# Causal mask of the attention scores: from accumulating mask products on TensorE to an add within VectorE's row maximum, with the score products of the two maps issued alternately

## The chip, the core and the metric

The kernel runs on one core of a Trainium2 chip. A core has a TensorE for matrix products (PE in the profile; its weight loads are PEld), a VectorE (DVE), a ScalarE (ACT), a GpSimd (POOL) and a SyncE (SP), which here issues most DMAs. Each engine takes its own instructions in order, and engines wait for one another by semaphores. Products land in PSUM, eight banks of 512 fp32 columns on 128 partitions; everything else lies in SBUF. The metric is the device time of one execution in microseconds, the median of several runs.

## What is computed

Two layers of a block over 256 tokens of 1024 features. Each layer has a mixer with three branches (spatial gating, a state space scan, differential attention), which are gated and merged, and a feed forward with a convolution. The change lies in the attention branch, four heads with two score maps each:

```python
def diff_attention(q, k, v, q_g, k_g, lam_vecs, subln_g, lam_init, cos, sin):
    ...
    def block(args):
        qb, bi = args
        scores = jnp.einsum('bqhmd,bkhmd->bhmqk', qb, kh)
        q_pos = bi * Q_BLOCK + jnp.arange(Q_BLOCK)
        mask = k_pos[None, :] <= q_pos[:, None]
        p = jax.nn.softmax(jnp.where(mask, scores, -jnp.inf), axis=-1)
        w = p[:, :, 0] - lam * p[:, :, 1]
        return jnp.einsum('bhqk,bkhd->bqhd', w, vf)
```

A head has 64 features in each map; queries are taken in two blocks of 128. The first block sees keys 0 to 127, the second keys 0 to 255, and in both only the last 128 x 128 square needs the causal mask.

## The kernel before

All weights stream through SBUF in half blocks of 128 x 1024 fp32. ScalarE writes the high part of each (`whi`, L231), VectorE the rest (`wlo`, L234), and every product with weights is three products of such parts (`mm3`, L276 to L278). `next_half` keeps four split half blocks ahead of the one in use; five buffers exist for each part. TensorE goes through the items of a layer in a fixed order: q, k, x B C, v, z, g, u, then gates and branches a, c and b (tiles `g_a`, `b_a`, `g_c`, `b_c`, `g_b`, `b_b`), the output projection (`wo`), and the feed forward (`up`, `acc`).

Everything that is not a stream of weights is written as a generator, whose steps are taken at each half block (`tick`), so many per half block as its rate says. `attention()` is one of them (rate 1.45). It runs beside the gates and branches, together with the state space scan `ssd()` (tiles `seg`, `y`, `xs`) and the spatial gating (`gm`, `gmy`). The framework then orders the instructions of each engine, so the order on an engine can differ a little from that of the text.

Attention goes through five stages for each head, and in one round of the loop at L650 a later stage of an earlier head comes before an earlier stage of a later head:

- `scores` (L581): for each map `m` and each query block a product of 64 rows of `qT` and `kT` into the PSUM tile of that map, columns 0 to 127 for the first block and 128 to 383 for the second. Map 0 lies on partitions 0 to 63 and map 1 on 64 to 127. Directly behind each product a second one, of `identb` (a bf16 identity) and `negb` (0 or -3e38, bf16), adds the mask to the last 128 columns (L590). TensorE takes an fp32 product in two passes, each with its weight load.
- `soft` (L593): VectorE takes four row maxima out of PSUM (L602) and scales them (L603); ScalarE takes four exponentials from PSUM into the SBUF tiles `pe` (L607), each with a row sum.
- `combine` (L613): VectorE makes p0 - lam * p1 with the sums (L617 to L624), in place in `pe`.
- `turn` (L630): TensorE turns three 128 x 128 squares of `pe` (tile `wt`, L633), ScalarE copies them out.
- `values` (L637): TensorE multiplies with `va` (tile `po`).

The `pe` tiles come from a ring of seven buffers of 2 KB (`s2`), which wT, gmy and others share. The PSUM tiles come from a ring of eight banks.

`identb` and `negb` are cast from the constants `cst` once, at the start (L406, L407). `cst` has 592 columns, the mask 128 of them (`K_NEG`).

Of the kernel before, what the change touches and what calls it, by code (L numbers as in the profile page):

```python
# [20 lines left out]
P = 128  # L21
# [9 lines left out]
# order of the mixer's input products: q, k, v, spatial gate g, u, x B C in pairs of tiles, z  # L31
MIX = ("q", "k", "x4", "x5", "v", "x0", "x1", "z0", "x2", "x3", "z1", "g", "u0", "u1")
# buffers of 4 KiB, of 2 KiB and of the split weights
NS4, NS2, NWB, AHEAD = 18, 7, 5, 4
HP = 200
# feed forward: hidden tile after which the down products start
# [7 lines left out]
# columns of w_in  # L44
# [3 lines left out]
# row constants of a layer  # L48
R_GMG, R_GMB, R_SSG, R_DTB, R_D, R_QK, R_SUB = 0, 512, 1024, 2048, 2064, 2080, 2208
R_N = 2336  # L50
# per-partition constants of a layer
PC_CW, PC_CB, PC_FW, PC_FB = 0, 48, 60, 60 + 6 * NFT
PC_N = PC_FB + 2 * NFT
# gains of the input norms, per layer: mixer, feed forward
G_N = 16
# constants that depend on shapes alone
K_ID, K_TRI, K_NEG, K_CC, K_SS = 0, 128, 256, 384, 416
K_II, K_REV = 448, 464
K_N = 592


def feat_block(w, c0, c1):
    """[1024, cols c0:c0+128 and c1:c1+128] -> [128, 2 tiles, 8 k, 128]"""
    a = w.reshape(8, P, -1)
    return np.stack([a[:, :, c : c + P].transpose(1, 0, 2) for c in (c0, c1)], 1).reshape(P, BLK)


def tok_blocks(w):
    """[K, 512 n] -> blocks of [128, 4 k, 512], the k halves of a column group together"""
    k, n = w.shape  # L70
    a = w.reshape(k // 512, 4, P, n // 512, 512).transpose(3, 0, 2, 1, 4)
    return list(a.reshape(-1, P, BLK))


def out_blocks(w):
    """[1024, 1024] -> blocks of [128, 4 tiles, 4 k, 128], halves of k outermost"""
    a = w.reshape(2, 4, P, 2, 4, P).transpose(0, 3, 2, 4, 1, 5)
    return list(a.reshape(-1, P, BLK))
# [41 lines left out]
def bc(ap, n):  # L120
    """append a broadcast dim of n"""
    return ap.unsqueeze(len(ap.shape)).to_broadcast([*ap.shape, n])
# [3 lines left out]
def block_kernel(ctx: ExitStack, tc: tile.TileContext, x, wstream, wdt, rows, prol, pcols, gains, gmw, consts, out):  # L126
# [20 lines left out]
    # the residual stream, features on partitions  # L147
# [13 lines left out]
    # the activation table is there before the data  # L161
# [3 lines left out]
    # the tensor engine's clock is up when the data comes  # L165
# [5 lines left out]

    identb = cpool.tile([P, P], BF16, name="identb")
    negb = cpool.tile([P, P], BF16, name="negb")
# [8 lines left out]
    def prologue():  # L182
        """lambda and -exp(a_log) of both layers"""
        nc.sync.dma_start(pr, prol.rearrange("(o l) f -> o l f", o=1).to_broadcast([P, L, 272]))
        for l in range(L):
            lv = pr[:, l, 0:256].rearrange("p (a b d) -> p a b d", a=2, b=2)
            nc.vector.tensor_tensor(lprod[:, 2 * l : 2 * l + 2, :], lv[:, :, 0, :], lv[:, :, 1, :], op=ALU.mult)
        nc.vector.tensor_reduce(lsum.rearrange("p l a -> p (l a)"), lprod, op=ALU.add, axis=AX.X)
        nc.scalar.activation(lexp, lsum, AF.Exp)
        nc.scalar.activation(aneg, pr[:, :, 256:272], AF.Exp)  # L190
        nc.vector.tensor_scalar(aneg, aneg, -1.0, None, op0=ALU.mult)
        nc.vector.tensor_tensor(neglam, lexp[:, :, 1], lexp[:, :, 0], op=ALU.subtract)
        for l in range(L):
            lam_init = 0.8 - 0.6 * math.exp(-0.3 * l)
            nc.vector.tensor_scalar(neglam[:, l : l + 1], neglam[:, l : l + 1], -lam_init, None, op0=ALU.add)

# [5 lines left out]
    def load_half():  # L202
        i, hf = divmod(stream["i"], 2)
        parts = 1
        if hf == 0:
            raw = wpool.tile([P, BLK], F32, tag="raw", name=f"raw{i}", bufs=3)
            if i == 0:
                # the first block and the tiles of x as they are needed
                for q in range(4):
                    cs = slice(q * 512, (q + 1) * 512)  # L210
                    nc.sync.dma_start(x_sb[:, 2 * q : 2 * q + 2, :], x[:, 2 * q : 2 * q + 2, :])
                    nc.sync.dma_start(raw[:, cs], wstream[i, :, cs])
            elif i == 1:
                for q in range(2):
                    cs = slice(q * HB, (q + 1) * HB)
                    nc.sync.dma_start(raw[:, cs], wstream[i, :, cs])
                nc.sync.dma_start(cst, consts)
            else:
                nc.sync.dma_start(raw, wstream[i])
            stream["raw"] = raw  # L220
# [17 lines left out]
    def next_half():  # L238
        """the next half block; those after it are split ahead"""
        while len(ready) <= AHEAD and stream["i"] < n_halves:  # L240
            load_half()
        return ready.popleft()
# [3 lines left out]
    def load_table(name):  # L246
        """the next activations in program order, with their table set in place"""
        table["ins"] = tc.keep_in_program_order(nc.scalar.preload_act_table_set(name)).ins

# [24 lines left out]
    def mm3(o, a_hi, a_lo, b_hi, b_lo, start, stop):  # L274
        """o += a.T @ b, operands as high + low parts of 12 bits"""
# [4 lines left out]
    def feat_half(o, h_hi, h_lo):  # L280
        """one tile of 128 features of h @ w, features on partitions: o [128, 256]"""
# [6 lines left out]
    def feat_pair(o, h_hi, h_lo):  # L288
        """two tiles, with the last features of h as late as can be"""
# [12 lines left out]
    def tok_group(name, act, nk, evac, between=None):  # L302
        """512 columns of a product, tokens on partitions: act(k, i) gives the high and low
        activations of token tile i, evac(i, psum) takes what comes out"""
# [14 lines left out]
    def rsqrt_mean(src, n, scale, name):  # L319
        """(src * scale + eps) ** -0.5"""  # L320
# [15 lines left out]
    def transpose_split(src, dst, name, nk, scale=1.0):  # L336
        """src [128 tokens, nk * 128] -> features on partitions, high and low parts;
        dst(k0, k1) gives where tiles k0 to k1 go"""
# [14 lines left out]
    def scaled_tile(k, g, h_hi, h_lo):  # L353
        """feature tile k of x times its gain, split; the norm's factor of a token is applied to
        what the products give"""
# [10 lines left out]
    def norm_factors(name, res):  # L366
        """1 / rms of x by token: res gets [128, 2] with tokens on partitions, half of it, and the
        same along a row"""
# [35 lines left out]
    def layer_constants(l):  # L404
        if l == 0:
            nc.vector.tensor_copy(identb, ident)  # L406
            nc.vector.tensor_copy(negb, cst[:, K_NEG : K_NEG + P])  # L407
# [23 lines left out]
    for l in range(L):  # L431
# [34 lines left out]
        def dt_raw():  # L466
# [20 lines left out]
            # one table set for both functions  # L487
# [3 lines left out]
            # softplus(x) = max(x, 0) + log1p(exp(-|x|))  # L491
# [8 lines left out]
            # what rounding 1 + e dropped, to first order  # L500
# [10 lines left out]
            # cumulative sums within chunks: by token, by head, and what is left to the end of chunk 0  # L511
# [63 lines left out]
        def attention():  # L575
# [5 lines left out]
            def scores(h):  # L581
                sc[h] = []
                for m in range(2):
                    o = ps(f"sc{l}_{h}_{m}")
                    ms = slice(64 * m, 64 * m + 64)
                    for i, (c0, n) in enumerate(spans):
                        nc.tensor.matmul(  # L587
                            o[:, c0 : c0 + n], qT[ms, h, i * P : (i + 1) * P], kT[ms, h, 0:n], start=True, stop=False
                        )
                        nc.tensor.matmul(o[:, c0 + n - P : c0 + n], identb, negb, start=False, stop=True)  # L590
                    sc[h].append(o)

            def soft(h):  # L593
                # columns: (tile 0, map 0), (tile 0, map 1), (tile 1, map 0), (tile 1, map 1)
# [4 lines left out]
                for m in range(2):  # L599
                    for i, (c0, n) in enumerate(spans):  # L600
                        q = 2 * i + m
                        nc.vector.tensor_reduce(mx[:, q : q + 1], sc[h][m][:, c0 : c0 + n], op=ALU.max, axis=AX.X)  # L602
                nc.vector.tensor_scalar(nmx, mx, -0.125, None, op0=ALU.mult)  # L603
                for m in range(2):
                    for i, (c0, n) in enumerate(spans):
                        q = 2 * i + m
                        nc.scalar.activation(  # L607
                            p[m][:, c0 : c0 + n], sc[h][m][:, c0 : c0 + n], AF.Exp,
# [4 lines left out]
            def combine(h):  # L613
                # weights over sum 0: p0 - lam * (sum0 / sum1) * p1
# [60 lines left out]
        def normed(o, row, name):  # L675
            """two feature tiles times the norm's factors"""
# [43 lines left out]
        def conv(u, y, wcol, bcol, taps, pcl):  # L720
            """causal depthwise convolution along the free axis"""
# [13 lines left out]
        def ssd_in():  # L735
            # B with tokens on partitions
# [7 lines left out]
            # C B^T, lower triangle, transposed  # L744
# [12 lines left out]
        def x_tokens(b):  # L757
            """half the heads with tokens on partitions: x, dt x, the skip term, and what chunk 0
            leaves to chunk 1"""
# [59 lines left out]
        def ssd():  # L819
# [13 lines left out]
            def decay(i, g):  # L833
                # exp(min(a_t - a_s, 0))
# [82 lines left out]
        # what can go beside the stream once these items are there  # L917
# [25 lines left out]
        # a gate is (tanh(x / 2) + 1) / 2; the half is taken where the merged sum is split  # L943
# [130 lines left out]
def shape_constants():  # L1074
# [6 lines left out]
    c[:, K_NEG : K_NEG + P] = np.where(r[None, :] <= r[:, None], 0.0, -3.0e38)  # L1081
# [77 lines left out]
```

## Time and profile before

| what | value |
|---|---|
| median of 3 runs | 973.7 us (973.24 to 974.42) |
| profiled execution: span from the first to the last instruction | 970.6 us |
| profiled execution: its own time beside the span | not listed; the median of the runs is 3.1 us above the span |
| instructions | 15931 |
| TensorE clock granted, mean | 0.998 |
| DMA | 172.71 MB, 178 GB/s over the span |

The page gives the busy time of each engine, the costliest groups of instructions with what ended the idle time before them, and the chain of work that ended last: followed back from the last instruction, at each step to what released it, or to the instruction before it on its engine. The time of the chain is what the kernel takes; idle time of an engine off the chain costs nothing. Ends of products are modelled, so the distance from start to start says more than a product's own duration. The chain can be read piece by piece in order of time, and its pieces are such distances.

### The profile page before, as it was taken

How to read it: one execution, taken by the hardware profiler on the slowest of the kernel's cores; microseconds unless marked ns; L12 is line 12 of the kernel's file. 1: busy time of each engine (PE TensorE's matmuls, PEld its weight loads, DVE VectorE, ACT ScalarE, POOL GpSimd, SP SyncE). 2: the span in 40 equal slices, each digit the busy share in tenths (PEclk: the TensorE clock that was granted, in tenths of full speed). 3: DMA queues.
4: the chain of work that ended last, by engine and by line, in shares of the span. 5: the costliest groups of instructions: out<-in, count | busy, mean ns of one | idle time of the engine just before them, and what ended most of it. 6: DMA issues, size and time to landing. Idle time of an engine off the chain costs nothing.

```text
span 970.6 us, 15931 instructions
## 1 busy us (share of the span) xinstructions
PE 961.9 (99%) x6465; PEld 877.5 (90%) x6465; DVE 714.7 (74%) x1072; ACT 572.9 (59%) x880; POOL 39.3 (4%) x48
## 2 busy tenths in 40 slices
PE   8999999999999999999999999999999999999998
PEld 5999787888899999999988988878888999999998
DVE  6698767667568978787677975776756788877774
ACT  6676577554445755555457666776544566555552
POOL 2020010000000000000001100000000000000000
PEclk9999999999999999999999999999999999999999
DMA  7854572347555555555544555633455545555541
GB/s 294 277 178 174 174 260 99 131 141 243 186 174 174 175 187 194 184 177 177 190 177 151 175 175 174 234 113 131 158 189 175 178 169 198 193 175 177 186 160 44
DMA packets 29145, 172.71 MB, mean 178 GB/s; under 512 B 5232, under 2 KB 6544, under 8 KB 9360
## 3 DMA queue, kind: packets, MB, share of 16 engines
q1 hardware_dynamic: 27712, 167.46, 49.9%
q0 software_dynamic: 1216, 4.23, 1.4%
q8 instruction: 50, 0.82, 0.3%
q14 instruction: 23, 0.19, 0.1%
q10 hardware_dynamic: 144, 0.02, 0.0%
HBM read 170.61 MB, written 1.08 MB: 177 GB/s over the span
## 4 chain that ended last, share of the span: by engine, by line
PE 98%; DMA 0%; POOL 0%; ACT 0%; DVE 0%; issue 0%; ACTq 0%; POOLq 0%
PE up L276 9%; PE up L277 9%; PE up L278 9%; PE acc L278 4%; PE acc L277 4%; PE acc L276 4%; PE xbc L276 2%; PE xbc L277 2%; PE xbc L278 2%; PE sc L587 2%; PE wo L278 2%; PE wo L277 2%; PE wo L276 2%; PE g_a L276 2%; PE g_a L277 2%; PE g_a L278 2%
## 5 line engine op out<-in xcount | busy, mean ns | idle before, releaser
L231 ACT ACTIVATE whi<-raw 128x1024 fp32r<-128x1024 f32 (+1 forms) x310 | 325.0, 1051 | 274.8 <-PE up L277 82.4
L234 DVE TENSOR_TENSOR wlo<-raw,whi 128x1024 fp32r<-128x1024 f32 (+1 forms) x310 | 375.8, 1216 | 148.1 <-ACT whi L231 145.5
L276 PE MATMUL up<-f_hi,whi 128*128 128x256 f32 x704 | 199.6, 283 | 0.0
L277 PE MATMUL up<-f_lo,whi 128*128 128x256 f32 x704 | 199.2, 283 | 0.0
L278 PE MATMUL up<-f_hi,wlo 128*128 128x256 f32 x704 | 199.2, 283 | 0.0
L277 PEld LDWEIGHTS up<-f_lo,whi 128*128 128x128 f32 x704 | 135.2, 192 | 0.0
L276 PEld LDWEIGHTS up<-f_hi,whi 128*128 128x128 f32 x704 | 135.2, 192 | 0.0
L278 PEld LDWEIGHTS up<-f_hi,wlo 128*128 128x128 f32 x704 | 135.1, 192 | 0.0
L276 PE MATMUL acc<-act,whi 128*128 128x256 f32 x352 | 99.6, 283 | 0.0
L277 PE MATMUL acc<-act,whi 128*128 128x256 f32 x352 | 99.6, 283 | 0.0
L278 PE MATMUL acc<-act,wlo 128*128 128x256 f32 x352 | 99.6, 283 | 0.0
L727 DVE SCALAR_TENSOR_TENSOR fy<-fu,pc,fy 128x254 f32<-128x254 f32 (+1 forms) x176 | 73.6, 478 | 0.2
L276 PEld LDWEIGHTS acc<-act,whi 128*128 128x128 f32 x352 | 67.6, 192 | 0.0
L277 PEld LDWEIGHTS acc<-act,whi 128*128 128x128 f32 x352 | 67.6, 192 | 0.0
L278 PEld LDWEIGHTS acc<-act,wlo 128*128 128x128 f32 x352 | 67.6, 192 | 0.0
L276 PE MATMUL xbc<-h_hi,whi 128*128 128x256 f32 x192 | 55.1, 287 | 0.0
L277 PE MATMUL xbc<-h_lo,whi 128*128 128x256 f32 x192 | 54.3, 283 | 0.0
L278 PE MATMUL xbc<-h_hi,wlo 128*128 128x256 f32 x192 | 54.3, 283 | 0.0
L722 ACT ACTIVATE fy<-fu,pc 128x256 f32<-128x256 f32 x88 | 47.7, 588 | 3.8 <-DVE fu L678 3.8
L328 ACT ACTIVATE act<-fy 128x256 fp32r<-128x256 f32 x44 | 18.3, 416 | 49.3 <-DVE fy L1023 49.3
L678 DVE TENSOR_TENSOR fu<-up,fn_row 128x512 f32<-128x512 f32 x44 | 30.2, 690 | 16.0 <-PE up L278 16.0
L277 PEld LDWEIGHTS xbc<-h_lo,whi 128*128 128x128 f32 x192 | 36.8, 192 | 0.1
(305 smaller groups left out, 1970.9 us busy)
## 6 DMA issues: line engine op xcount, KB each, us to landing
raw<-in_wstream SPq DMA_DIRECT2D x152, 1024.0 KB, 4.9
seg<-scr POOLq DMA_DIRECT2D x8, 512.0 KB, 7.0
rows<-in_rows SPq DMA_DIRECT2D x2, 1168.0 KB, 7.9
x_sb<-in_x SPq DMA_DIRECT2D x4, 256.0 KB, 4.5
raw<-in_wstream SPq DMA_DIRECT2D x4, 256.0 KB, 4.7
raw<-in_wstream SPq DMA_DIRECT2D x2, 512.0 KB, 6.7
out_x<-x_sb SPq DMA_DIRECT2D x8, 128.0 KB, 1.8
gmw<-in_gmw SPq DMA_DIRECT2D x2, 256.0 KB, 6.0
```

The costliest lines, as they stand in the source:

```text
L231: split = nc.scalar.activation(hi[:, cs], src[:, cs], AF.Copy)
L234: nc.vector.tensor_tensor(lo[:, cs], src[:, cs], hi[:, cs].bitcast(F32), op=ALU.subtract)
L276: nc.tensor.matmul(o, a_hi, b_hi, start=start, stop=False)
L277: nc.tensor.matmul(o, a_hi, b_lo, start=False, stop=False)
L278: nc.tensor.matmul(o, a_lo, b_hi, start=False, stop=stop)
L328: nc.scalar.activation(dst_hi, src, AF.Copy, scale=scale)
L587: nc.tensor.matmul(o[:, c0 : c0 + n], qT[ms, h, i * P : (i + 1) * P], kT[ms, h, 0:n], start=True, stop=False)
L678: nc.vector.tensor_tensor(u, o.rearrange("p (m t) -> p m t", m=2), row.unsqueeze(1).to_broadcast([P, 2, S]), op=ALU.mult)
L722: nc.scalar.activation(y, u, AF.Identity, bias=pcl[:, bcol : bcol + 1], scale=pcl[:, wcol + taps - 1 : wcol + taps])
L727: nc.vector.scalar_tensor_tensor(y[:, d:], u[:, : S - d], pcl[:, w : w + 1], y[:, d:], op0=ALU.mult, op1=ALU.add)
```

## The change

The mask products and their two bf16 constants go. The score products are ordered by query block first and map second, so that successive products take map 0 and map 1 in turn; each is a complete product by itself. VectorE's row maximum becomes `tensor_tensor_reduce`: it reads the scores from PSUM and the mask from SBUF, writes their sum to the `pe` tile, and gives its row maximum (scale 1.0, start value -3e38). The exponential reads the `pe` tile and writes over it. The mask in the constants is 256 columns wide, 128 of zero and then the triangle, so that one slice of it fits either query block; `cst` grows from 592 to 720 columns. Comments are removed everywhere, which changes nothing that runs.

```diff
-K_ID, K_TRI, K_NEG, K_CC, K_SS = 0, 128, 256, 384, 416
-K_II, K_REV = 448, 464
-K_N = 592
+K_ID, K_TRI, K_NEG, K_CC, K_SS = 0, 128, 256, 512, 544
+K_II, K_REV = 576, 592
+K_N = 720
...
-    identb = cpool.tile([P, P], BF16, name="identb")
-    negb = cpool.tile([P, P], BF16, name="negb")
...
-        if l == 0:
-            nc.vector.tensor_copy(identb, ident)
-            nc.vector.tensor_copy(negb, cst[:, K_NEG : K_NEG + P])
...
             def scores(h):
-                sc[h] = []
-                for m in range(2):
-                    o = ps(f"sc{l}_{h}_{m}")
-                    ms = slice(64 * m, 64 * m + 64)
-                    for i, (c0, n) in enumerate(spans):
+                sc[h] = [ps(f"sc{l}_{h}_{m}") for m in range(2)]
+                for i, (c0, n) in enumerate(spans):
+                    for m in range(2):
+                        ms = slice(64 * m, 64 * m + 64)
                         nc.tensor.matmul(
-                            o[:, c0 : c0 + n], qT[ms, h, i * P : (i + 1) * P], kT[ms, h, 0:n], start=True, stop=False
+                            sc[h][m][:, c0 : c0 + n], qT[ms, h, i * P : (i + 1) * P], kT[ms, h, 0:n],
+                            start=True, stop=True,
                         )
-                        nc.tensor.matmul(o[:, c0 + n - P : c0 + n], identb, negb, start=False, stop=True)
-                    sc[h].append(o)
...
-                        nc.vector.tensor_reduce(mx[:, q : q + 1], sc[h][m][:, c0 : c0 + n], op=ALU.max, axis=AX.X)
+                        nc.vector.tensor_tensor_reduce(
+                            p[m][:, c0 : c0 + n], sc[h][m][:, c0 : c0 + n], cst[:, K_NEG + 2 * P - n : K_NEG + 2 * P],
+                            1.0, -3.0e38, op0=ALU.add, op1=ALU.max, accum_out=mx[:, q : q + 1],
+                        )
...
-                            p[m][:, c0 : c0 + n], sc[h][m][:, c0 : c0 + n], AF.Exp,
+                            p[m][:, c0 : c0 + n], p[m][:, c0 : c0 + n], AF.Exp,
                             bias=nmx[:, q : q + 1], scale=0.125, accum_out=sums[:, q : q + 1],
...
-    c[:, K_NEG : K_NEG + P] = np.where(r[None, :] <= r[:, None], 0.0, -3.0e38)
+    c[:, K_NEG + P : K_NEG + 2 * P] = np.where(r[None, :] <= r[:, None], 0.0, -3.0e38)
```

## The prediction

> **What bounds the kernel now.** I read the busy table of the page and the summary of the chain that ended last, then all waits of TensorE.
>
> ```profile
> PE 961.9 (99%) x6465; PEld 877.5 (90%) x6465; DVE 714.7 (74%) x1072; ACT 572.9 (59%) x880; POOL 39.3 (4%) x48
> PE 98%; DMA 0%; POOL 0%; ACT 0%; DVE 0%; issue 0%; ACTq 0%; POOLq 0%
> PE an_rb L389 <- POOL an_rp L324: 2.6, 2, 2.3
> PE warm L170 <- DVE cold L167: 1.2, 1, 1.2
> PE q L276 <- ACT whi L231: 0.7, 1, 0.7
> ```
>
> TensorE is the whole path: 98% of the chain, and only 4.5 us of waits for others in 970.6 us, none in attention. A microsecond that leaves TensorE's stream therefore leaves the end, as long as no other engine becomes late. Next comes the chain piece by piece (start, length in us, what) at one head's scores, with the pieces around it.
>
> ```profile
> 138.16 0.23 PE g_a L278
> 138.38 0.42 PE sc L587 x2
> 138.80 0.16 PE sc L590
> 138.96 0.63 PE sc L587 x2
> 139.59 0.16 PE sc L590
> 139.75 0.41 PE sc L587 x2
> 140.16 0.16 PE sc L590
> 140.33 0.63 PE sc L587 x2
> 140.95 0.16 PE sc L590
> 141.12 0.28 PE g_a L276
> 141.40 0.24 PE g_a L277
> ```
>
> A score call (L587) is two passes ("x2"), with 128 or with 256 columns; behind each stands one mask product (L590). The head holds TensorE from 138.38 to 141.12, and the gate product behind it takes 0.28 where its neighbours take 0.23: 2.79 us. Eight heads (4 in each of 2 layers) make 22.3 us. How much of that is work shows in places where passes of the same kind follow one another without a change of tile:
>
> ```profile
> 146.65 0.89 PE gm L706 x8
> 97.01 0.86 PE st L787 x2
> 33.17 0.54 PE pdt L477 x4
> 33.71 0.43 PE k L278
> 34.14 0.23 PE k L276
> ```
>
> gm: 8 fp32 passes of 128 columns, 0.89 / 8 = 0.111 each. st: 2 passes of 512 columns, 0.43 each, so 0.215 for 256. A score call would then be 0.22 or 0.43; it takes 0.42 or 0.63. **0.20 us are added to every call**, whatever its length. The next view says by what: the tile of an instruction stands before its shape.
>
> ```profile
> L587 PE MATMUL sc<-kT,qT x64: 272/374/690, 138.3 to 648.1; 64*128 64x128 f32 x32, 64*128 64x256 f32 x32
> L590 PE MATMUL sc<-negb,identb x32: 229/229/286, 138.7 to 648.4; 128*128 128x128 bf16 x32
> ```
>
> Scores use half the array's rows (tile 64*128), masks all of them (128*128). The tile changes eight times a head, and k behind pdt, which also returns from a smaller tile, shows the same price: 0.43 against 0.23, again 0.20.
>
> **The change part by part.**
>
> *Masks removed.* 32 L590 products go, 0.16 us of the chain each: 0.64 us a head.
>
> *Four calls in a row.* Without masks only two changes of tile remain per head, into 64*128 and out of it. Work: 2 x (2 x 0.111) + 2 x (2 x 0.215) = 1.30. Changes: 2 x 0.20 = 0.40. So 1.70 us where 2.79 stood, **1.09 saved**; 8 x 1.09 = 8.7 us, of which 5.1 are the masks (8 x 0.64) and 3.6 the changes of tile. What the trace doesn't show is one call directly behind another on the other half of the rows (map 0 uses rows 0 to 63, map 1 rows 64 to 127). Bounds: 0.20 lost at each of these three junctions, as at a change of tile (+0.60 a head); or the second pass of one call running beside the first of the next, which hides at most 0.111 + 0.111 + 0.215 = 0.44 a head. The nearest row is pdt: four small-tile passes behind one another, 0.54 with the way in, no gap and no overlap. I take zero. Both ends return as rivals.
>
> *Maximum with the mask on VectorE.* Per head four reductions (L602) become four two-source operations that also write the masked scores to SBUF. The nearest rows:
>
> ```profile
> L602 DVE TENSOR_REDUCE mx<-sc 128x1 f32<-128x256 f32 x8 | 3.3, 412 | 0.0
> L602 DVE TENSOR_REDUCE mx<-sc 128x1 f32<-128x128 f32 x8 | 2.3, 283 | 1.9 <-PE sc L590 1.9
> L624 DVE SCALAR_TENSOR_TENSOR pe<-pe,cf,pe 128x256 f32<-128x256 f32 x3 | 1.4, 480 | 0.0
> L624 DVE SCALAR_TENSOR_TENSOR pe<-pe,cf,pe 128x128 f32<-128x128 f32 x3 | 1.0, 348 | 0.0
> L607 ACT ACTIVATION_READ_ACCUMULATOR pe<-sc,nmx 128x1 f32 x12 | 2.4, 204 | 0.0
> ```
>
> At best it costs what the reduction does, at worst a two-source operation (0.07 more) and a separate reading of the accumulator as ScalarE has it (0.20): 0 to 0.27 us each, 0 to 1.1 a head. No row has this operation. I take 0.07, by its two sources, and on the path nothing, because VectorE's lead covers it:
>
> ```profile
> L234 DVE TENSOR_TENSOR wlo<-raw,whi 128x1024 fp32r<-128x1024 f32 x8 | 9.8, 1221 | 5.0 <-ACT whi L231 4.9
> L231 ACT ACTIVATE whi<-raw 128x1024 fp32r<-128x1024 f32 x9 | 9.5, 1060 | 6.2 <-PE g_a L278 5.2 <-PE u L277 0.9
> ```
>
> In attention (this view is of 136 to 176 us) the split of the next weights waits for TensorE to free a buffer (6.2 us of waits), so it is always as far ahead as five buffers allow. When TensorE leaves one half block, four lie before it, of 12 products of 0.23 us: 4 x 2.76 = 11.0 us. The new split takes 1.06 + 1.22 of them; 8.7 us of lead remain. Only a delay beyond that reaches the path.
>
> *An earlier buffer.* The masked maximum writes into the pe tile, which until now only the exponential wrote. For a layer's fourth head that tile is the one that the turn of its second head still reads. Its three steps now:
>
> ```profile
> 170.77 0.28 DVE L602 TENSOR_REDUCE mx<-sc 128x1 f32<-128x128 f32 x1
> 179.11 0.49 PE L633 MATMUL wt<-cst,pe 128*128 128x128 f32 x3
> 180.65 0.36 ACT L607 ACTIVATE pe<-sc,nmx 128x128 f32<-128x128 f32 x1
> ```
>
> The maximum will have to wait for the turn (179.11 + 0.49), 8.8 us later than it ran. Behind it in VectorE's queue stand combine of the third head, the state space sums and the next weight splits, and behind those TensorE. 8.8 against 8.7 of lead: nothing, or some tenths if the order on VectorE stays as it is; nothing at all if other work is put ahead. Cost 0, at worst, with four operations (1.4) behind the wait, 8.8 + 1.4 - 8.7 = 1.5 us a layer, 3 in all. The PSUM banks of the scores come free no later than now, after the exponential at 180.65.
>
> *Exponential in place.* It reads SBUF instead of PSUM:
>
> ```profile
> L607 ACT ACTIVATE pe<-sc,nmx 128x128 f32<-128x128 f32 x6 | 2.2, 362 | 0.1
> L839 ACT ACTIVATE seg<-seg,acum 128x128 f32<-128x128 f32 x29 | 9.3, 392 | 0.0
> ```
>
> By L839, SBUF to SBUF, 0.03 more each, 0.12 a head on an engine with the same lead: nothing.
>
> *Start.* Two casts leave VectorE; the constants grow by 128 columns, 64 KB.
>
> ```profile
> cst<-in_consts SPq DMA_DIRECT2D x1, 296.0 KB, 7.4
> ```
>
> 7.4 us for 296 KB makes at most 1.6 for 64 KB, if nothing overlaps, in a queue where weights follow. Its first reader on TensorE (the row factors, the 2.6 us wait above) comes late, and waits for POOL. I take 0, with 0 to 1.6 as bounds.
>
> **Sum.** 8.7 us off TensorE, 0 elsewhere. Only the span of the profiled execution is shown, 970.6; it becomes 961.9. The median of the three runs, 973.7, lies 3.1 above that span, and I leave this distance as it is: 973.7 - 8.7 = **965.0 us**.
>
> One more thing moves by itself, the granted clock:
>
> ```profile
> 160.40:163.90 3.50, 3.50 (x11) 2.46 (x12) 3.50 (x7) 1.70 (x7) 0.52 (x1) 0.51 0.61 255
> ```
>
> The third column from the end (0.51) is TensorE's clock: once, behind a stretch of state space products and a head's scores, it stood at half for 3.5 us, which costs 1.7. Seven other heads passed without. Shorter score stretches should make this rarer, but where it falls can change: 0, 1 or 2 such windows, 963.3 to 966.7.
>
> **The rivals.**
>
> *The halves overlap.* Consecutive calls use different rows and different PSUM banks, so passes can run side by side. If only the long one can (0.215 a head): 1.7 us more, 963.3; if all three junctions do (0.44): 3.5 more, 961.5. Against it: no row shows two products at once. Chance 0.33.
>
> ```profile
> 138.31 0.29 PEld L587 LDWEIGHTS sc<-kT,qT 64*128 64x128 f32 x2 [0.35 <-issue]
> ```
>
> The Trainium skill, "TensorE: Matmul & The Clock Gate", Part 3 (The mechanism), says that matmuls in different row groups start some 4 ns apart and run concurrently; by it the time would be 961.5. It adds that a weight load overlaps a running matmul only where the row group differs. There the row above disagrees: two loads of the same half take 0.29 together though each lasts 0.18, the second beginning while the first pass streams.
>
> *A change of half costs as much as a change of tile.* Then alternating maps gives five changes of 0.20 a head: 1.30 + 1.00 = 2.30, 0.49 saved, 3.9 in all: 969.8. The alternation would hold back most of what removing the masks gives. For it: every place where the rows in use change in this trace costs 0.20. Against it: in all of them the tile's size changes too. Chance 0.11. The Trainium skill, "TensorEngine Tiling (Array Packing)", Key Properties, says that changing the tiling mode, not just the tile, drains TensorE; the 0.20 rows agree with the first half, and by the second this rival would fall away.
>
> *VectorE's wait reaches the path* (the earlier buffer, with or without the constants): up to 3 + 1.6 given back, 965 to 969.6. Chance 0.08; the lead speaks against it.
>
> *Slower: the clock.* Masks work on the whole array; without them a head's scores are 1.7 us of products on half its rows. If each of the other seven stretches lost a window as the one at 160.40 did, 7 x 1.7 = 11.9: 973.7 - 8.7 + 11.9 = 976.9. It decides from the sixth extra window on (5.1 x 1.7 = 8.7). Against it: 7 of 8 longer stretches kept the clock. Chance 0.04.
>
> **How the numbers follow.** Forecast 965.0 with zero to two clock windows: 0.44. The range, 961.0 to 968.0, covers it, nearly all of the overlap and most of VectorE's wait; outside are the costly change of half (0.11), the clock (0.04) and small rests of the others (0.05). A difference of 0.2% (1.9 us) is about what can be told from no change. All but the clock lie below 971.8; with a little for several small losses together: faster 0.93, same 0.03, slower 0.04.
>
> **What would show it.** In the chain, four score pieces without mask pieces, 0.22 + 0.22 + 0.43 + 0.43 and 0.20 on either side; overlap shows as less than 1.30, a costly change of half as about 2.1. The new operation on VectorE at 0.29 to 0.55 us and no new wait of TensorE for wlo. The granted clock says which windows were lost. I am wrong if the chain leaves TensorE in attention, or if TensorE's pieces elsewhere grow.

## The result, and the profile after

The changed kernel takes **955.96 us** (median of 4 runs, 955.67 to 956.79) where the kernel before took 974.06 beside it (973.24 to 975.27): a ratio of 0.9814, with a 95% interval of 0.9800 to 0.9828. The gain is 18.1 us. Forecast were 8.7 us and 965.0; the measured time lies 5.0 us below the lower end of the range. The direction was right, and so was the engine from which the time would leave; the forecast gain was about half of what came.

The first lines of the page of the changed kernel: its span, the busy time of each engine, and the summary of the chain that ended last. Behind them stand all waits of TensorE (what waited, for whom, us in total, times, longest).

```profile
span 954.7 us, 15887 instructions
PE 947.4 (99%) x6433; PEld 868.3 (91%) x6433; DVE 714.5 (75%) x1102; ACT 572.6 (60%) x880; POOL 40.0 (4%) x48
PE 97%; DMA 1%; DVE 0%; ACT 0%; POOL 0%; issue 0%; SPq 0%; ACTq 0%; POOLq 0%
```

```profile
PE warm L170 <- DVE cold L167: 1.2, 1, 1.2
PE q L273 <- ACT whi L228: 0.8, 1, 0.8
PE an_rb L386 <- POOL an_rp L321: 0.6, 2, 0.4
PE q L274 <- DVE wlo L231: 0.4, 1, 0.4
PE k L274 <- DVE wlo L231: 0.2, 1, 0.2
```

TensorE is still the whole path, and nothing in attention makes it wait. VectorE is as busy as before (714.5 us against 714.7), though it now adds the mask. One wait has shrunk: `an_rb`, in the start of the kernel, from 2.6 to 0.6 us. No part of the change was meant for it.

The same head's scores as in the prediction, in the chain piece by piece (start, us, what):

```profile
137.69 0.23 PE g_a L275
137.92 0.86 PE sc L581 x8
138.77 0.43 PE g_a L273
139.20 0.23 PE g_a L274
```

The eight passes of a head hold TensorE for 0.86 us, the way in included, and the gate product behind them takes 0.43 where its neighbours take 0.23: 0.86 + 0.20 = 1.06 us, where 2.79 stood. The forecast was 1.70. Eight heads make 8 x 1.73 = **13.8 us**, of which 8 x 1.09 = 8.7 had been foreseen and 8 x 0.64 = 5.1 had not. The rest of the 18.1, some 4 us, came from the start and from the granted clock, in neither of which I had expected a gain. The experiments take the three apart.

### The profile page after: what moved, and what is told of

Its sections match the earlier page's. It is cut to its first block, busy times and chain, and to the rows that moved or that the text cites. A ratio compares the mean times of both kernels' runs of the same rounds, so it can differ in the third digit from the quotient of the medians.

```text
span 954.7 us, 15887 instructions
## 1 busy us (share of the span) xinstructions
PE 947.4 (99%) x6433; PEld 868.3 (91%) x6433; DVE 714.5 (75%) x1102; ACT 572.6 (60%) x880; POOL 40.0 (4%) x48
## 4 chain that ended last, share of the span: by engine, by line
PE 97%; DMA 1%; DVE 0%; ACT 0%; POOL 0%; issue 0%; SPq 0%; ACTq 0%; POOLq 0%
PE up L273 9%; PE up L274 9%; PE up L275 9%; PE acc L275 4%; PE acc L274 4%; PE acc L273 4%; PE xbc L273 2%; PE xbc L274 2%; PE xbc L275 2%; PE g_a L273 2%; PE wo L274 2%; PE wo L273 2%; PE wo L275 2%; PE z L275 2%; PE g_c L273 2%; PE g_c L275 2%
```

## The experiments

Each differs from the changed kernel ("after") or from the kernel before in the lines shown. Beside the first four the kernel before took 974.68 us, beside the kernel before with `rh` put ahead 974.36, beside the others 974.06.

**One half for both maps.** If calls on different halves of TensorE's rows run side by side, then calls on one half must show the time of the forecast. Here both maps use rows 0 to 63, so that the second map gets the first one's scores; the work is the same.

```diff
-                        ms = slice(64 * m, 64 * m + 64)
+                        ms = slice(0, 64)
```

> The changed kernel, but the score products of both maps read partitions 0 to 63 (map 1 gets map 0's features, so its scores are not the reference's); same instructions, shapes and order. Theory A, two score calls on different halves of the array's rows run wholly side by side: they can't here, so eight passes take 4 x 0.111 + 4 x 0.215 = 1.30 us behind one another, with the way in 1.50 in the chain instead of 0.86, 8 x 0.64 = 5.1 us more than the changed kernel: about 961. Theory B, the halves don't matter and passes of 64 rows are just faster when no mask product stands between: 0.86 as before, about 956.

Measured: 961.43 us (961.07 to 962.0), 5.5 more than after. Its chain at the same head:

```profile
137.20 0.23 PE g_a L275
137.43 1.50 PE sc L581 x8
138.93 0.43 PE g_a L273
```

1.50 + 0.20 = 1.70 us: the forecast's sum to the hundredth. 8 x 0.64 = 5.1 of the 5.5 us are the overlap that this kernel lacks. The weight loads of that head show the overlap directly, in the timeline (start, us from the first to the last end, engine, line, how many), first after, then this kernel:

```profile
137.85 0.52 PEld L581 LDWEIGHTS sc<-kT,qT 64*128 64x128 f32 x8 [0.35 <-issue]
```

```profile
137.35 1.17 PEld L581 LDWEIGHTS sc<-kT,qT 64*128 64x128 f32 x8 [0.35 <-issue]
```

Each load lasts some 0.18 us; eight of them begin and end within 0.52 us on two halves, and within 1.17 on one. Taken one by one, the products of after start in pairs: at 137.848 and 137.855, at 138.062 and 138.068, at 138.173 and 138.180, at 138.392 and 138.398. Within a pair they are 6 to 7 ns apart, and from pair to pair 0.11 to 0.22 us. So not the second pass of one call runs beside the first of the next, as my bound had it: **whole calls run side by side**, pass for pass. One map's work, 2 x 0.111 + 2 x 0.215 = 0.65, disappears behind the other's. The Trainium skill, "TensorE: Matmul & The Clock Gate", Part 3 (The mechanism), has matmuls of different row groups start some 4 ns apart and run concurrently. The trace agrees that they run side by side; the distance here is 6 to 7 ns.

**Map outside, query block inside.** After's alternation undone, the masks still gone.

```diff
-                for i, (c0, n) in enumerate(spans):
-                    for m in range(2):
+                for m in range(2):
+                    for i, (c0, n) in enumerate(spans):
```

> The changed kernel with the two loops of the score products exchanged: both query blocks of map 0, then both of map 1. Theory A: only the 256-column call of map 0 and the 128-column call of map 1 are neighbours on different halves; 0.22 + 0.43 + 0.43 = 1.08 less the hidden part, about 0.86 + 0.20 = 1.06 in the chain, 8 x 0.2 = 1.7 us more than the changed kernel: 957.6. Theory B: 0.86, about 956. If only the second pass of a call can run beside the first pass of the next (rival of the prediction): about 1.3, some 959.5.

Measured: 956.48 us (956.42 to 957.03), 0.5 above after, and the same piece in the chain:

```profile
137.76 0.86 PE sc L581 x8
138.62 0.43 PE g_a L273
```

What I had expected of the theory that proved right, 957.6 and an overlap only where neighbours in the queue use different halves, was wrong. In the trace the first two products of 128 columns start at 137.692 and 137.705, two more of them at 137.905 and 137.918, and only then those of 256 columns, at 138.017 and 138.030. By the program, map 0's call of 256 columns stands ahead of map 1's of 128. The framework could have changed that order, but the semaphore marks in the traces speak against it. I read `+=` as a product's report for several calls at once and `++` as one for its own call. In after, and with one half for both maps, the first call of 256 columns is marked `+=` and the second `++`; here both are marked `+=`, as in before, where map 0 also came first as a whole. So the call of the free half started past a call that waited for its own half: each half takes its calls in order, but not the two halves together, and the first section's sentence that each engine takes its instructions in order doesn't hold for these calls. The same section of the Trainium skill says that products start strictly in program order; these starts don't agree. In this kernel, then, the **alternation brings nothing once the masks are gone**.

**Masks kept, calls paired.** The kernel before with its mask products, but both maps' calls of a query block first and their two masks behind them.

```diff
-                for m in range(2):
-                    o = ps(f"sc{l}_{h}_{m}")
...
-                    for i, (c0, n) in enumerate(spans):
+                for i, (c0, n) in enumerate(spans):
+                    for m in range(2):
...
-                        nc.tensor.matmul(o[:, c0 + n - P : c0 + n], identb, negb, start=False, stop=True)
+                    for m in range(2):
+                        nc.tensor.matmul(sc[h][m][:, c0 + n - P : c0 + n], identb, negb, start=False, stop=True)
```

> The kernel before with its mask products kept, but the two maps issued alternately: for each query block two score calls, then two masks; VectorE and ScalarE as before. Theory A: per head (0.20 + 0.22 + 0.22) + (0.20 + 0.43 + 0.22) + 0.05 = 1.54 instead of 2.79, 8 x 1.25 = 10 us off: about 964. Theory B or no overlap: (0.20 + 0.44 + 0.22) + (0.20 + 0.86 + 0.22) + 0.05 = 2.19, 4.8 us off: about 969.

Measured: 963.18 us (961.93 to 963.64), ratio to before 0.9882 (0.9868 to 0.9895). A head of it in the chain:

```profile
140.33 0.42 PE sc L586 x4
140.75 0.22 PE sc L591 x2
140.97 0.63 PE sc L586 x4
141.60 0.22 PE sc L591 x2
141.82 0.29 PE g_a L276
```

Two calls now take what one took before (0.42 and 0.63). A head costs 0.42 + 0.22 + 0.63 + 0.22 + 0.06 = 1.55 us: 1.24 less than before, 0.49 more than after. Here the order does matter: between masks, which use the whole array, calls overlap only if they stand together. So 9.9 of the 13.8 us (8 x 1.24) are to be had with the masks in place.

**Plain reduction.** After's score calls, but before's reduction and exponential, both from PSUM; the mask is left out altogether.

```diff
-                        nc.vector.tensor_tensor_reduce(
...
+                        nc.vector.tensor_reduce(mx[:, q : q + 1], sc[h][m][:, c0 : c0 + n], op=ALU.max, axis=AX.X)
...
-                            p[m][:, c0 : c0 + n], p[m][:, c0 : c0 + n], AF.Exp,
+                            p[m][:, c0 : c0 + n], sc[h][m][:, c0 : c0 + n], AF.Exp,
```

> The changed kernel's score products with VectorE and ScalarE as before: a plain row maximum from PSUM, exponential from PSUM; the causal mask is left out, so the weights are not the reference's. If VectorE's new operation costs nothing on the path: as the changed kernel within 0.7 us, 955.3 to 956.7. If it delays something: faster than that by over 1 us. If the earlier release of the scores' banks is part of the gain: slower by over 1 us.

Measured: 956.29 us (955.91 to 956.71). Adding the mask on VectorE and the exponential in place neither cost nor gain anything on the path that shows (0.3 us beside after). What they cost off it, in after's groups of the same stretch as in the prediction (136 to 176 us; busy us, mean ns, idle time before):

```profile
L596 DVE CUSTOM_DVE_ANT_0 pe<-sc,cst 128x256 f32<-128x256 f32 x8 | 3.3, 417 | 0.0
L604 ACT ACTIVATE pe<-pe,nmx 128x128 f32<-128x128 f32 x7 | 2.7, 392 | 0.0
L596 DVE CUSTOM_DVE_ANT_0 pe<-sc,cst 128x128 f32<-128x128 f32 x8 | 2.3, 286 | 1.4 <-PE sc L581 1.4
L596 DVE DVE_READ_ACCUMULATOR2_ANT mx<- 128x1 f32 x16 | 1.3, 83 | 0.0
```

The new operation takes 286 and 417 ns where the reduction took 283 and 412, and then 83 ns to read its maximum.

**The start.** After's `an_rb` wait is 2 us shorter. VectorE's order in the start differs: `rh` (`an_rh`, L392) stands ahead of the two weight splits (`wlo`) in after, behind them before. Theory S: while VectorE splits weights, GpSimd's two small operations on `an_r` take longer, and TensorE waits for them. The timelines, before and then after:

```profile
18.88 2.36 DVE L234 TENSOR_TENSOR wlo<-raw,whi 128x1024 fp32r<-128x1024 f32 x2
19.05 1.11 POOL L322 TENSOR_SCALAR an_r<-an_s 128x2 f32<-128x2 f32 x1 [18.17 <-DVE an_s L384]
20.24 1.57 POOL L324 TENSOR_TENSOR an_rp<-an_r,mhalf 128x2 f32<-128x2 f32 x1
21.87 0.71 PE L389 MATMUL an_rb<-cst,an_rp 128*128 128x128 f32 x4 [2.29 <-POOL an_rp L324]
```

```profile
19.95 0.19 POOL L319 TENSOR_SCALAR an_r<-an_s 128x2 f32<-128x2 f32 x1 [19.07 <-DVE an_s L381]
20.22 0.71 POOL L321 TENSOR_TENSOR an_rp<-an_r,mhalf 128x2 f32<-128x2 f32 x1
20.97 0.89 DVE L392 TENSOR_SCALAR an_rh<-an_rp 128x2 f32<-128x2 f32 x1 [1.11 <-POOL an_rp L321]
21.05 2.36 DVE L231 TENSOR_TENSOR wlo<-raw,whi 128x1024 fp32r<-128x1024 f32 x2
```

In after VectorE stands still for 1.11 us until `an_rp` is there, and GpSimd needs 0.19 and 0.71 us; beside the splits it needed 1.11 and 1.57. Two kernels test this: after with `rh` put back behind the row's copy, and before with `rh` put ahead.

```diff
-        nc.vector.tensor_copy(row, t2[:, 0:S])
+        copied = nc.vector.tensor_copy(row, t2[:, 0:S])
...
-        nc.vector.tensor_scalar(rh, r[:, 0:2], 0.5, None, op0=ALU.mult)
+        with tc.issue_after(copied.ins):
+            nc.vector.tensor_scalar(rh, r[:, 0:2], 0.5, None, op0=ALU.mult)
```

> The changed kernel, with VectorE's half of the row factor (an_rh) held behind the copy of the factors along a row, as it stood in the kernel before; in between VectorE now runs weight splits while GpSimd works on the factors. Theory S, the start became shorter because VectorE stands still while GpSimd works: GpSimd's two steps go back from 0.19 and 0.71 us to about 1.1 and 1.6, TensorE's wait for them from 0.6 to about 2.6, 1 to 2 us more than the changed kernel (and perhaps a half-clock window of 1.7 behind the wait): 957 to 959. Rival, the shorter start comes from the two casts that are gone or is chance: 956.0.

Measured: 959.19 us (957.78 to 959.86), 3.2 more than after. One line of its timeline, one of its waits:

```profile
20.76 1.57 POOL L321 TENSOR_TENSOR an_rp<-an_r,mhalf 128x2 f32<-128x2 f32 x1
```

```profile
PE an_rb L386 <- POOL an_rp L321: 2.4, 2, 2.1
```

Before's slow GpSimd steps and its wait are back. 1.8 us of wait (2.4 against 0.6) explain only part of 3.2; the rest is probably the clock (below).

```diff
-        nc.vector.tensor_scalar(rh, r[:, 0:2], 0.5, None, op0=ALU.mult)
+        with tc.high_priority(HP):
+            nc.vector.tensor_scalar(rh, r[:, 0:2], 0.5, None, op0=ALU.mult)
```

> The kernel before, its half of the row factor (an_rh) moved by a priority to between the two weight splits that VectorE runs while GpSimd works on the factors; masks and scores as before. Theory S: GpSimd's second step falls from 1.57 to 0.71 us, TensorE's wait from 2.6 to about 1.7, 0.9 off; if the half-clock window behind that wait goes as well, 1.7 more: 974.5 becomes 971.9 to 973.6. Rival, the start has nothing to do with this order: 974.5 as before.

Measured: 971.82 us (970.89 to 974.8, 8 runs), ratio to before 0.9980 (0.9968 to 0.9991): 2.5 us faster than before, where theory S and one window had been good for 2.6 at most. `rh` came to stand between the two splits, not ahead of both, so that only the second GpSimd step was freed:

```profile
19.50 1.23 DVE L234 TENSOR_TENSOR wlo<-raw,whi 128x1024 fp32r<-128x1024 f32 x1
19.68 1.11 POOL L322 TENSOR_SCALAR an_r<-an_s 128x2 f32<-128x2 f32 x1 [18.79 <-DVE an_s L384]
20.86 0.71 POOL L324 TENSOR_TENSOR an_rp<-an_r,mhalf 128x2 f32<-128x2 f32 x1
```

```profile
PE an_rb L389 <- POOL an_rp L324: 1.8, 2, 1.4
```

The step beside the split ends at 19.68 + 1.11 = 20.79, 0.06 us after the split (19.50 + 1.23 = 20.73); the next one, beside none, takes 0.71. GpSimd was held until the split was over. The Trainium skill, "SBUF — State Buffer", section "SBUF: two separate sides", states this: a VectorE operation with two inputs in SBUF holds the port pair that it shares with GpSimd for the whole instruction, against a GpSimd operation that reads SBUF, and the other is blocked. The trace agrees, here and in before (first split 18.88 + 1.23 = 20.11, GpSimd's step until 20.16).

Why the order on VectorE changed at all was tried once. After, with the two casts back in their old place, though nothing reads them:

```diff
+        if l == 0:
+            nc.vector.tensor_copy(identb, ident)
+            nc.vector.tensor_copy(negb, cst[:, K_NEG + P : K_NEG + 2 * P])
```

> The changed kernel with the two casts of identity and mask to bf16 put back at the start; nothing reads them. Theory S: an_rh still stands ahead of the splits on VectorE, so GpSimd's steps stay at 0.19 and 0.71 us: 956.0 within 0.5. Rival, the casts themselves are what made the start longer: 957 to 959.

Measured: 956.22 us (956.01 to 956.48), with after's quick GpSimd steps. It isn't the casts. It isn't the new maximum either, since the plain reduction above also has after's start (wait 0.6), while the kernel with the masks kept has before's (2.6). Which of the remaining parts moved `rh`, the mask products or the wider constants, stays open.

**The kernel before once more, for its clock.** The profile of before showed one stretch at half clock. Theory C: most executions of before have more than one. Nothing is edited here; the same kernel is profiled once more and run ten times.

> The kernel before, unchanged, for a second profile. Theory C, it loses one to three windows of half clock in most executions, at changing places, 1.7 us each, and the changed kernel none: granted clock 0.996 to 0.998, spans 970.7 to 973.5 in step with it. Rival: the spans differ for another reason, with the clock alike.

Measured: 974.73 us (972.74 to 975.0, 10 runs). The profiled execution, 972.6 us long, has two such stretches. The view gives, for each stretch, the busy time of each engine (with instructions), and then TensorE's granted clock, the DMA share and GB/s:

```profile
20.00:23.10 3.10, 0.82 (x6) 0.71 (x6) 1.76 (x2) 0.73 (x2) 3.02 (x3) 1.00 0.42 167
23.10:26.50 3.40, 3.40 (x9) 2.61 (x9) 3.27 (x4) 2.84 (x4) 1.39 (x2) 0.50 0.56 84
26.50:30.00 3.50, 3.50 (x16) 2.87 (x16) 0.90 (x3) 0.64 (x1) 0.00 (x0) 1.00 0.99 384
159.00:163.00 4.00, 4.00 (x25) 2.85 (x24) 4.00 (x8) 3.61 (x9) 1.44 (x1) 1.00 0.49 145
163.00:166.40 3.40, 3.40 (x12) 2.80 (x12) 3.19 (x6) 2.24 (x7) 0.05 (x1) 0.50 0.51 214
```

One lies right behind the stretch in which TensorE did 0.82 us of work in 3.10, because it waited for `an_rb`; the other behind a head's scores, as the one at 160.40 in the first profile. Each costs 1.7 us. TensorE waits 2.6 us for `an_rb` in this execution, as in the first profile. The spans of the ten executions go with the mean clock: 970.6 and 970.9 at 0.998, 971.4 at 0.997, seven of 972.5 to 972.9 at 0.996. The execution whose profile the prediction read was thus among the quickest, by its clock one window short of seven of these ten. After has none at either place:

```profile
20.00:30.00 10.00, 9.56 (x44) 7.33 (x43) 6.48 (x8) 6.19 (x7) 4.12 (x4) 1.00 0.80 284
158.00:168.00 10.00, 10.00 (x60) 8.26 (x59) 9.25 (x19) 8.44 (x22) 0.33 (x1) 1.00 0.28 102
```

The window behind the start goes with the wait for `an_rb`: of the four profiles with a wait of 2.4 or 2.6 us, this one and that with masks kept (22.6 to 26.0) have it, the first of before and that with `rh` put back don't; none of the seven with a wait of 1.8 or less has it. With `rh` put back the three executions that weren't profiled have a mean clock of 0.997 or 0.998. If they lost it behind the start, which only a profile could show, that accounts for the 3.2 us: 1.0 to 2.2 of start (the span of 955.7 without a window against after's 953.5 to 954.7), and 1.7 for the window in three runs of four.

Why the same wait brings a window or not is suggested by the clock records of the traces, though no run could move them at will. In each of the eleven profiles all changes of TensorE's clock lie whole multiples of 3.413 us apart (here 163.02 - 23.08 = 139.94, 41 of them), on a grid that begins at another place of the program in each execution. With the two windows behind the start, the wait falls into one piece of the grid, in which TensorE is busy for 1.1 of 3.4 us (19.66 to 23.08 here, 19.18 to 22.59 with masks kept); in the first profile of before and with `rh` put back the grid divides it (busy 2.5 and 2.0 us; 2.9 and 1.9). Ahead of the windows at 160 and 163 TensorE counts as busy, but the products that start in that piece have 2368 and 2432 columns together, where half of after's pieces have 7168 or more and its poorest 3840. That isn't the whole condition: three pieces with 2176 to 2304 columns (in this profile and in that with `rh` put ahead) were followed by full clock.

**Two heads at once.** Each change of tile still costs 0.20, twice a head. Issuing the scores of two heads together should save one pair of changes in two.

```diff
-                        stages[j](t - j)
+                        if j:
+                            stages[j](t - j)
+                        elif t % 2 == 0:
+                            scores(t)
+                            scores(t + 1)
```

> The changed kernel with the scores of two heads issued together, so that the tile changes in and out of 64*128 once for two heads. If each way in and each way out costs 0.20: 4 x 0.40 = 1.6 us less than the changed kernel, 954.4; 16 passes in the chain take about 0.20 + 1.28. If the way out is hidden or four banks held at once make TensorE wait: 956 or more.

Measured: **954.73 us** (954.02 to 954.77), ratio to before 0.9799 (0.9785 to 0.9814). It is the quickest of all kernels run: 1.2 us below after, and 1.5 below the kernel with the casts put back, which ran beside it. Its chain:

```profile
137.43 1.51 PE sc L581 x16
138.94 0.43 PE g_a L273
```

1.51 + 0.20 for two heads, where after takes 2 x 1.06 = 2.12: 0.41 saved for each of four pairs, 1.6 us.

## Why the prediction was wrong, point by point

**What bounds the kernel**: right. All that left TensorE's stream left the end, and the chain stayed on TensorE throughout attention.

**"Masks removed" and "Four calls in a row"**: their sum was right, 8.7 us. The kernel with one half for both maps saves just this, and its head takes the 1.70 us that were worked out. The division into 5.1 of masks and 3.6 of tile changes was not: with masks kept, two masks behind one another take 0.22 where one took 0.16, so a mask itself adds 0.06, and the other 0.10 of each 0.16 go with the change of tile. **The step that failed** is the junction between calls on different halves: "I take zero", with 0.44 a head as the most that overlap could give. It gave 0.64, or 5.1 us in all. Both choices erred in one way. Zero was taken from pdt as the nearest row, but pdt's passes all use the same rows of the array (0 to 31, by its code), so they said nothing of calls that use different ones; they also have 16 columns each, and not the 128 or 256 of a score call. And the bound was worked out for passes following one another in a single queue, where only neighbours can meet; what is side by side is the halves, and the bound of that is all the work of one half, 0.65. The rival "the halves overlap" was the right mechanism, at a price of 3.5 where it brought 5.1; it and the Trainium skill's sentence on row groups deserved more than a chance of 0.33, as no row spoke against products side by side on two halves.

**"A change of half costs as much as a change of tile"**: refuted. In after the half changes within every pair, and the pair costs what one call costs.

**"Maximum with the mask on VectorE"** and **"Exponential in place"**: right on the path (nothing; the plain reduction shows it), and close off it. The maximum cost 3 to 5 ns and 83 of reading more than the reduction, where 70 were taken; the exponential at 392 ns is the 0.03 us more that were taken.

**"An earlier buffer"**: the price was nothing, as taken, but the wait isn't shown. In after's timeline VectorE's maxima of layer 0's fourth head stand late, among the weight splits:

```profile
171.48 1.23 DVE L231 TENSOR_TENSOR wlo<-raw,whi 128x1024 fp32r<-128x1024 f32 x1 [1.95 <-ACT whi L228]
172.62 0.42 DVE L596 CUSTOM_DVE_ANT_0 pe<-sc,cst 128x256 f32<-128x256 f32 x1
```

They run 7 to 11 us behind the scores (162). The first wrote its tile at 169.23, ahead of the turn of the second head (170.19 in after), so it didn't wait for it; the other three stood behind a split that had itself waited 1.95 us for ScalarE. No wait of TensorE for `wlo` appears in attention. The rival "VectorE's wait reaches the path" falls.

**"Start"**: taken as 0, bounded by a loss only. It was a gain. The larger constants cost nothing that shows; VectorE's new order freed GpSimd, and TensorE's wait fell by 2.0 us. What failed is that the start was costed by what the diff adds there, and not by what the rest of the change may do to the order of the engines' queues.

**The clock**: the range allowed for zero to two windows in the changed kernel, but compared them with a before of one. By their mean clock more than half of the executions of before have two (0.996), and after has none (0.999 or 1.0), so up to 3.4 us went. The rival "slower: the clock" had the sign wrong: the shorter score stretches lost no window, and the wait that preceded the other one is gone.

**Median and profile**: the distance of 3.1 us between the profiled span and the median was not a distance. A run's time lies a constant 2.1 us above its own span (956.79 and 954.7 in after); the other 1.0 was that the profiled execution of before was shorter than most, because it lost fewer windows.

The account, from the runs: before to masks kept 974.68 - 963.18 = 11.5 us, of which 9.9 are scores; the rest, 1.6, is a remainder of about the size of one window, the one at 160. From there to after 7.2 us, of which 8 x 0.49 = 3.9 are scores and 3.2 the start with the window behind it. In sum 13.8 of scores, 3.2 of start with its window, 1.6 of the other window: 18.6, beside 18.1 to 18.7 measured.

What stays open: what exactly decides on the window at 160. It stood behind the state space products and scores in both profiles of before, and after's shorter scores make that place richer in columns; but before with `rh` put ahead, whose scores and masks are unchanged, has no window in its profile and a mean clock of 0.999 or 1.0 in four of eight executions, which none of the 44 executions of before with a listed clock reached. So a shifted start alone can avoid it, and some of its 1.7 us may belong to the start and not to the scores. No run varied the state space products alone. Whether the halves overlap when both maps write one PSUM bank wasn't tried.

## What to carry to other kernels

Where two operands each fill half of TensorE's rows, put their calls together and keep full-array products out from between them; the bound of the gain is all the work of one half, plus 0.20 us for each change of tile avoided. Before a forecast is set against one profile, take several executions, and ask of each half-clock window what TensorE did in the 3.4 us ahead of it and whether the change touches that. And compare the engines' orders in the start: small GpSimd steps on the path want VectorE's two-input operations behind them, not beside them.

## What the runs showed that I had not expected

- Calls on the free half overtake calls that wait for their own half: the map-outer kernel takes 0.86 us a head, the same as the alternating one.
- GpSimd's operations on 128 x 2 elements take 0.19 and 0.71 us alone, 1.11 and 1.57 beside VectorE's splits; the first ends less than 0.1 us behind a split, the second 0.57 (20.24 + 1.57 = 21.81 against 18.88 + 2.36 = 21.24). Spans of GpSimd are rough, but TensorE's wait moved with them, from 0.6 to 2.6.
- A wait of 2.1 to 2.3 us of TensorE in the start was followed by 3.4 us at half clock in two of four profiles: the same wait can cost 1.7 us more or nothing, it seems by where it falls on the grid of 3.413 us.
